# Plain DMAs on the SP queue for the last two stores of a sliding-window kernel, from late buffers

## The chip, the cores and the metric

One core of one Trainium2 chip. The metric is the device time of one execution in microseconds (us). Lower is better.

The names are the profile's. ACT (ScalarE) and DVE (VectorE) copy here; POOL (GpSimd), SP (SyncE) and ACT have queues on which they issue DMAs, which are q0, q1 and q10 in the page. The bytes are moved by 16 DMA engines, packet by packet, between the on-chip buffers and HBM, the memory that holds input and output. A store lands when its last completion is seen. POOL's closing drain is an instruction near the end of the program; in the traces it begins about when POOL issues its last store.

## The reference

```python
# x: (16, 64, 64, 64) float32, window 8, stride 4  ->  out: (16, 15, 15, 64, 8, 8)
for i in range(n_h):                     # n_h = n_w = 15
    for j in range(n_w):
        result[:, i, j] = x[:, :, 4*i:4*i+8, 4*j:4*j+8]
```

It is all copying: 16.8 MB are read and 59 MB are written. In the output one row, of one batch `b`, one window `(i, j)` and one half `ch` of the channels, is 2048 floats, 8 KB in a row. The two halves are neighbours, so a window of one batch is 16 KB.

## The kernel before

Partition `p` holds `(b, ch, q)`, that is 8b + 4ch + q, where `q` is a quarter of the image's rows. A window step `(j, s)` copies, for every partition, the window with `i = 4q + s` into a store buffer and stores the buffer's 128 rows by one indirect DMA of POOL's queue. ACT copies for `s` < 3; for `s` = 3 the window reaches into the next quarter, so DVE copies half and shuffles the other half in from the neighbouring partition. For `s` = 3 the quarter `q` = 3 has no window, and its index is out of bounds on purpose.

```python
UNITS = 18                                     # nine buffers of 1 MB (128 x 2048 f32)
G = gpool.tile([P, UNITS * HCL, WS, WS], f32, name="G")
at = 0
def window(j, s, half):
    # ... u = at % UNITS; at += n        (n = 2 for a whole buffer)
    g = G[:, u * HCL : (u + n) * HCL, :, :]
    if not last:
        nc.scalar.copy(out=g, in_=L[:, cs, s * ST : s * ST + WS, cols])
    else:
        nc.vector.tensor_copy(out=g[:, :, 0:ST, :], in_=L[:, cs, s * ST : RB, cols])
        nc.vector.stream_shuffle(out=g[:, :, ST:WS, :], in_=L[:, cs, 0:ST, cols], mask=nxt)
    # ...
    st = nc.gpsimd.indirect_dma_start(out=o, out_offset=..., in_=g..., ...)
    # ... stores are declared independent of each other
# ... early windows by halves, then
for w in rest:
    window(*w, None)
```

I count stores from the end: store -1 is the last one (`s` = 3, 96 rows), -2 the one before it (`s` = 2, 128 rows).

## Time and profile before

| | before |
|---|---|
| median, lowest to highest | 194.41 us, 194.27 to 194.75 (6 runs, with those beside the changed kernel) |
| span in the profile | 192.4 us |
| last landing of a store | 188.6 us |
| POOL's long drain ends | 191.6 us |

Times within the profile are us from the start of the span. The prediction below shows the lines of the page, of the end in windows and of the closing instructions.

### The profile page before, as it was taken

To read this page: it belongs to the slowest core of one execution; us is meant where nothing else is said; L and a number is where in the kernel's file an instruction comes from. 1 tells how busy PE (TensorE), PEld (TensorE's weight loads), DVE (VectorE), ACT (ScalarE), POOL (GpSimd) and SP (SyncE) were. 2 spreads that over 40 slices of the span, in tenths; PEclk is the share of its full clock that TensorE was granted. 3 is DMA by queue.
4 is the path that set the end of the run, shared out by engine and by line. 5 is a ranking of instruction groups with operands and counts; after the bars stand their busy time and mean duration, and the time that the engine had idled before them with its cause. 6 is when DMAs were issued, how large, how long until landed. Compare 5 with 4: busy or idle time off the path is not lost.

```text
span 192.4 us, 478 instructions
## 1 busy us (share of the span) xinstructions
DVE 30.4 (16%) x65; ACT 86.2 (45%) x55; POOL 70.3 (37%) x77
## 2 busy tenths in 40 slices
DVE  2000050000232302303030122121121203030000
ACT  0000049500699875373747465646565655600000
POOL 0000027723367766456363253434343434440000
DMA  5999999999999999999999999999999999999960
GB/s 183 418 413 410 410 410 414 417 417 422 420 421 427 429 414 429 404 403 418 412 409 409 419 404 409 416 405 409 409 412 409 409 411 412 407 409 414 424 257 17
DMA packets 14724, 75.80 MB, mean 394 GB/s; under 512 B 1984, under 2 KB 1984, under 8 KB 8960
## 3 DMA queue, kind: packets, MB, share of 16 engines
q0 software_dynamic: 10368, 58.99, 75.3%
q1 hardware_dynamic: 2176, 8.39, 11.0%
q10 hardware_dynamic: 2176, 8.39, 10.8%
q14 instruction: 4, 0.03, 0.0%
HBM read 16.78 MB, written 62.91 MB: 414 GB/s over the span
## 4 chain that ended last, share of the span: by engine, by line
DMA 65%; issue 19%; ACT 3%; POOL 1%; POOLq 1%; PEldq 0%
DMA out_dram<-G,idx_last 38%; DMA out_dram<-G,idx 14%; DMA out_dram<-G,idx_h 8%; DMA out_dram<-G,idx_hlast 6%; ACT G L101 3%; POOL out_dram L109 1%; POOLq L165 1%; POOLq L109 0%; POOL pi L61 0%; PEldq L165 0%
## 5 line engine op out<-in xcount | busy, mean ns | idle before, releaser
L101 ACT COPY G<-L 128x2048 f32<-128x2048 f32 (+1 forms) x54 | 84.9, 1613 | 54.4 <-DMA out_dram<-G,idx 18.6
L109 POOL DMA_INDIRECT out_dram<-G,idx x36 | 34.8, 966 | 47.0 <-DMA out_dram<-G,idx 43.1
L103 DVE COPY G<-L 128x1024 f32<-128x1024 f32 (+1 forms) x18 | 11.1, 618 | 138.3 <-DMA out_dram<-G,idx 62.8
L109 POOL DMA_INDIRECT out_dram<-G,idx_h x18 | 17.4, 966 | 13.9 <-DMA out_dram<-G,idx_hlast 4.3
L104 DVE STREAM_SHUFFLE G<-L 128x1024 f32<-128x1024 f32 (+1 forms) x18 | 19.6, 1090 | 0.0
L109 POOL DMA_INDIRECT out_dram<-G,idx_hlast x6 | 5.9, 990 | 27.9 <-DVE G L104 26.4
L109 POOL DMA_INDIRECT out_dram<-G,idx_last x12 | 11.8, 986 | 11.7 <-DVE G L104 6.8
L101 ACT ACT_TABLE_LOAD x1 | 1.3, 1283 | 26.6 <-DMA L<-in_x_dram 26.6
L62 DVE TENSOR_SCALAR tb<-pi 128x1 int32<-128x1 int32 x1 | 0.2, 155 | 1.0 <-POOL pi L61 1.0
L61 POOL IOTA pi<- 128x1 int32 x1 | 0.1, 120 | 0.4 <-PEq L165 0.4
L104 DVE LOAD_MASK_SELECT G<-L x18 | 0.2, 14 | 0.0
L151 POOL MEMSET const-float32-0.0<- 128x1 f32 x1 | 0.1, 100 | 0.2 <-issue 0.2
L68 DVE CUSTOM_DVE_ANT_0 idx<-tb,tc 128x2 uint16<-128x2 uint16 x1 | 0.2, 160 | 0.0
L66 DVE CUSTOM_DVE_ANT_0 tb<-tb,tc 128x2 uint16<-128x2 uint16 x1 | 0.2, 159 | 0.0
L67 DVE TENSOR_SCALAR tc<-tq 128x1 int32<-128x1 int32 x1 | 0.2, 154 | 0.0
L77 DVE TENSOR_SCALAR idx_hlast<-idx_last 128x1 int32<-128x1 int32 x1 | 0.2, 154 | 0.0
L77 DVE TENSOR_SCALAR idx_h<-idx 128x1 int32<-128x1 int32 x1 | 0.2, 154 | 0.0
L71 DVE CUSTOM_DVE_ANT_0 idx_last<-idx,tq 128x2 uint16<-128x2 uint16 x1 | 0.2, 153 | 0.0
L65 DVE TENSOR_SCALAR tb<-tb 128x1 int32<-128x1 int32 x1 | 0.2, 152 | 0.0
L70 DVE TENSOR_SCALAR tq<-tq 128x1 int32<-128x1 int32 x1 | 0.1, 148 | 0.0
L64 DVE TENSOR_SCALAR tq<-pi 128x1 int32<-128x1 int32 x1 | 0.1, 145 | 0.0
L63 DVE TENSOR_SCALAR tc<-pi 128x1 int32<-128x1 int32 x1 | 0.1, 144 | 0.0
(3 smaller groups left out, 0.3 us busy)
## 6 DMA issues: line engine op xcount, KB each, us to landing
L<-in_x_dram ACTq DMA_DIRECT2D x8, 1024.0 KB, 21.1
L<-in_x_dram SPq DMA_DIRECT2D x8, 1024.0 KB, 19.8
out_dram<-G,idx POOLq DMA_INDIRECT x36, 18.2
out_dram<-G,idx_h POOLq DMA_INDIRECT x18, 13.6
out_dram<-G,idx_last POOLq DMA_INDIRECT x12, 18.3
out_dram<-G,idx_hlast POOLq DMA_INDIRECT x6, 13.1
```

Source lines behind the costliest of these rows:

```text
L62: nc.vector.tensor_scalar(out=tb[:, :], in0=pi[:, :], scalar1=3, scalar2=None, op0=ALU.logical_shift_right)
L65: nc.vector.tensor_scalar(out=tb[:, :], in0=tb[:, :], scalar1=float(NWIN * CH), scalar2=None, op0=ALU.mult)
L66: nc.vector.tensor_tensor(out=tb[:, :], in0=tb[:, :], in1=tc_[:, :], op=ALU.add)
L67: nc.vector.tensor_scalar(out=tc_[:, :], in0=tq[:, :], scalar1=float(NSLOT * NW * CH), scalar2=None, op0=ALU.mult)
L68: nc.vector.tensor_tensor(out=idx[:, :], in0=tb[:, :], in1=tc_[:, :], op=ALU.add)
L71: nc.vector.tensor_tensor(out=idx_last[:, :], in0=idx[:, :], in1=tq[:, :], op=ALU.add)
L77: nc.vector.tensor_scalar(out=d[:, :], in0=e[:, :], scalar1=2.0, scalar2=None, op0=ALU.mult)
L101: nc.scalar.copy(out=g, in_=L[:, cs, s * ST : s * ST + WS, cols])
L103: nc.vector.tensor_copy(out=g[:, :, 0:ST, :], in_=L[:, cs, s * ST : RB, cols])
L104: nc.vector.stream_shuffle(out=g[:, :, ST:WS, :], in_=L[:, cs, 0:ST, cols], mask=nxt)
L109: st = nc.gpsimd.indirect_dma_start(out=o, out_offset=bass.IndirectOffsetOnAxis(ap=ix[:, 0:1], axis=0), in_=g.rearrange("p c r w -> p (c r ...
L165: with _tile.TileContext(nc) as tc:
```

## The change

The intent: the last two stores leave by plain DMAs of the SP queue, four for store -2 and three for store -1, one for each quarter `q`. Their buffers are those of stores -5 and -4, so their copies wait until those have landed. The nine buffers become nine tiles.

```diff
+    TAIL, BACK = 2, 3
+    o_q = out.rearrange("b i j (ch cl) r w -> i j b ch (cl r w)", ch=CH)
...
-    G = gpool.tile([P, UNITS * HCL, WS, WS], f32, name="G")
+    G = [gpool.tile([P, 2 * HCL, WS, WS], f32, name=f"G{n}") for n in range(UNITS // 2)]
...
-        g = G[:, u * HCL : (u + n) * HCL, :, :]
+        g = G[u // 2][:, u % 2 * HCL : (u % 2 + n) * HCL, :, :]
...
+        if (j, s) in order[-TAIL:]:
+            g_q = g.rearrange("(m q) c r w -> q m (c r w)", q=HQ)
+            for q in range(HQ - 1 if last else HQ):
+                free(nc.sync.dma_start(out=o_q[q * NSLOT + s, j], in_=g_q[q]))
+            return
...
-    for w in rest:
+    for w in rest[:-TAIL]:
+        window(*w, None)
+    at -= 2 * BACK
+    for w in rest[-TAIL:]:
         window(*w, None)
```

More of the change, by code (lines that the diff above doesn't have):

```diff
@@ L80, with free @@
     nxt = [min(p + 1, 31) for p in range(32)]
+    order = [(j, s) for j in range(NW) for s in range(NSLOT)]
+    TAIL, BACK = 2, 3
+    o_q = out.rearrange("b i j (ch cl) r w -> i j b ch (cl r w)", ch=CH)
+    def free(st):
+        tc.declare_no_dep(st.ins, group="stores", reason="each store writes rows of its own")
+        tc.add_to_no_dep_group("stores", st.ins)
     UNITS = 18
-    G = gpool.tile([P, UNITS * HCL, WS, WS], f32, name="G")
+    G = [gpool.tile([P, 2 * HCL, WS, WS], f32, name=f"G{n}") for n in range(UNITS // 2)]
     at = 0
@@ L117, in window @@
         )
-        tc.declare_no_dep(st.ins, group="stores", reason="each store writes rows of its own")
-        tc.add_to_no_dep_group("stores", st.ins)
-    order = [(j, s) for j in range(NW) for s in range(NSLOT)]
+        free(st)
     EARLY = 12
```

## The prediction

> **What bounds the kernel now.** I read the page's slices first, then the end of the run in windows, then the store issues one by one with their times to landing, then what stands after the last store. The page of the kernel before:
>
> ```profile
> DMA  5999999999999999999999999999999999999960
> GB/s 183 418 413 410 410 410 414 417 417 422 420 421 427 429 414 429 404 403 418 412 409 409 419 404 409 416 405 409 409 412 409 409 411 412 407 409 414 424 257 17
> ```
>
> One slice is 192.4/40 = 4.81 us. From slice 2 to slice 38 the 16 DMA engines are full at some 410 GB/s, so the body is bound by bytes, and the change moves the same bytes. Only the last two slices are free of that bound: 257 and 17 GB/s. The change can act there alone. The same stretch in windows (start:end, length, busy of DVE, ACT and POOL, clock, DMA share, GB/s):
>
> ```profile
> 183.00:184.00 1.00, 0.00 (x0) 0.00 (x0) 0.00 (x0) 1.00 0.97 401
> 184.00:185.00 1.00, 0.00 (x0) 0.00 (x0) 0.00 (x0) 1.00 0.57 238
> 185.00:186.00 1.00, 0.00 (x0) 0.00 (x0) 0.00 (x0) 1.00 0.48 205
> 186.00:187.00 1.00, 0.00 (x0) 0.00 (x0) 0.00 (x0) 1.00 0.47 197
> 187.00:188.00 1.00, 0.00 (x0) 0.00 (x0) 0.00 (x0) 1.00 0.51 213
> 188.00:189.00 1.00, 0.00 (x0) 0.00 (x0) 0.00 (x0) 1.00 0.01 0
> 192.00:193.00 1.00, 0.00 (x0) 0.00 (x0) 0.00 (x0) 1.00 0.00 0
> ```
>
> Two things end the run. From 184 to 188 a share of one half works: eight engines have finished and eight are about 4 us behind. Then from 188.3 to 192.4 no byte moves at all. What stands there is in the list of the closing line of the program (line 165; durations in ns min/median/max, then first and last start):
>
> ```profile
> L165 SPq EVENT_SEMAPHORE  x11: 17/28/28, 188.6 to 192.3; - x11
> L165 POOLq EVENT_SEMAPHORE  x4: 17/17/17, 191.6 to 192.3; - x4
> L165 POOLq DRAIN  x3: 40/107/21281, 170.3 to 192.1; - x3
> L165 SPq DRAIN  x3: 7/7/7, 189.2 to 191.9; - x3
> ```
>
> SP begins to see the completions at 188.6 and its drain is done at 189.2. POOL's drain, begun at 170.3, lasts 21.28 us, to 191.6; the closing barrier follows it (191.6 to 192.4). So POOL's drain ends 2.4 us later than SP's, and about 3.0 us after the last landing. The last landing, from the issue list of the final store:
>
> ```profile
> L109 POOL DMA_INDIRECT out_dram<-G,idx_last x1: 966/966/966, 170.5 to 170.5; - x1
> DMA to landing us min/median/max: 18.1/18.1/18.1
> ```
>
> 170.5 + 18.1 = 188.6. I count stores from the end: this is store -1. In the same way the fifth from the end, store -5, and stores -4 and -3:
>
> ```profile
> L109 POOL DMA_INDIRECT out_dram<-G,idx_last x1: 966/966/966, 161.1 to 161.1; - x1
> DMA to landing us min/median/max: 18.2/18.2/18.2
> ...
> L109 POOL DMA_INDIRECT out_dram<-G,idx x1: 966/966/966, 163.6 to 163.6; - x1
> DMA to landing us min/median/max: 18.3/18.3/18.3
> ...
> L109 POOL DMA_INDIRECT out_dram<-G,idx x1: 966/966/966, 166.0 to 166.0; - x1
> DMA to landing us min/median/max: 18.3/18.3/18.3
> ```
>
> They land at 179.3, 181.9 and 184.3. All is issued by 170.5 and a store takes 18 us to land, eight stores of some 2.5 us each: there is a deep backlog on the engines when POOL has nothing left to do.
>
> **What the Trainium skill says.** "DMA: Bandwidth & Descriptors", section "Issuing engines are not separate DMA queues": DMAs of all issuing engines run on the same 16 engines and interleave. The trace agrees as far as the loads go: they came from two queues and still made 410 to 418 GB/s together. So the SP queue brings no bandwidth. Same page, "Queues, rings and completion order": each DMA engine takes turns between queue rows packet by packet; no run here shows it yet, and I use it for store -3 below. Same page, "Why a DMA increments its semaphore by 16 and not by 1": the engines used by a DMA are the largest number up to 16 that divides the slowest dimension of both sides; here 32 partitions and 16 batches give 16, so plain stores load all engines alike and do not relieve the slow eight. The first-byte latency of 0.6 us for a plain DMA ("Specifications") is less than the trace has: the first load is issued at 0.74 and the first bytes move just after 2.1, so I take 1.4 us. No page that I found says what POOL's drain waits for.
>
> **The change part by part.** *Removed*: two indirect issues on POOL (0.97 us each), which lie under a full DMA queue and are worth nothing by themselves. But with them the last thing that POOL's drain has to wait for becomes store -3. *Tiles*: nine tiles in place of slices of one; same bytes, same depth; in the trace the copies already wait for their own slice, so I give it 0. *Moved*: the copies of stores -2 and -1 must now wait for stores -5 and -4 to land, not for stores nine back. That looks like a loss; its use is that it holds these two behind the POOL queue. Timetable:
>
> 1. Store -5 lands at 179.3; the ACT copy (1.90 us for this form) ends at 181.3. SP issues four plain DMAs of 256 KB; issue of one load took 0.60 us on SP and they followed each other by 0.65, so 181.35 to 183.95. First bytes at 181.35 + 1.4 = 182.8.
> 2. Store -4 lands at 181.9; DVE copy 0.69 + shuffle 1.28 (their rows at 167.9) end at 183.9, just as SP is free. Three DMAs (the fourth has no rows), issued 183.95 to 185.25; last bytes arrive on the queue at 186.7.
> 3. The eight fast engines run out at about 180 (4 us before the others) and idle to 182.8: lost, but they are not the last. They end near 186.7 + 0.6 = 187.3.
> 4. The eight slow engines never idle: at 182.8 they hold 1.2 us of store -3, then 8 + 6 packets of 8 KB. At 418/16 = 26.1 GB/s one packet is 0.314 us, so 182.8 + 1.2 + 14 x 0.314 = 188.4, landing 0.3 later as before: 188.7. Against 188.6 before: nothing gained or lost.
> 5. Store -3 shares the slow engines with store -2 from 182.8; its 1.2 us can double at most, so it lands by about 185.5. If POOL's drain ends 3.0 us after the last landing of its own queue, it ends at 188.5, ahead of SP.
> 6. The end is now SP's: 188.7 + 0.64 (its row of waits, 188.6 to 189.2, as before) = 189.3, plus the closing barrier 192.4 - 191.6 = 0.8: 190.1 to 190.2 in place of 192.4.
>
> Sum: POOL's drain off the end -2.4, the two landings about +0.1: -2.2 to -2.3 us. If SP's wait for the last DMA happens to be late in its row, up to 0.5 more. Time: 194.4 - 2.3 = 192.1 us.
>
> **The rivals.** *The late start costs more than it gives.* If the first bytes of a plain DMA take 3 us, or an SP issue of this shape 1 us, the last DMA reaches the engines after 187.8 and the slow eight idle too: then each us later is a us of the run, and 193 to 195 comes out. For it: the chain landing, copy, issue is serial twice. Against: a slack of 188.4 - 0.6 - 186.7 = 1.1 us by the timetable. *POOL's drain doesn't follow its own queue's last landing* but something else of fixed length or all queues: then the end stays at 191.6 + 0.8 and the time at 194.4. For it: the trace doesn't say what it waits for; against: it outlasts the last landing by 3 us, while another POOL drain took 107 ns. *Rebalancing*: if the plain DMAs gave the idle eight more of the bytes, half of the 4 us lag could go, 2 us more: 190.1. Against: 16 divides both sides, equal shares. *Store -3 is starved by the SP queue* on the slow engines and lands at 187 or later: POOL's drain then ends at 190 and the gain is 1.5 or less: 193.
>
> **Range and chances.** The mechanism with its spread (SP's wait order -0.5, issue and first bytes +1) gives 191.5 to 193.2; the rivals widen it upwards. I predict 192.1 us, with 191.3 to 193.6 as the range for 8 in 10. Two per cent is 3.9 us: under 190.5 only the rebalancing helps, 4 in 100; over 198.3 would need 4 us of idle slow engines, 2 in 100; within 2%, 94 in 100.
>
> **What would show it.** Step 1: ACT's last copy starts near 179.4 and waits for a store with the last-row index. Step 2: DVE's last copy near 181.9. Step 3 and 4: DMA share about one half from 180 to 183, full or nearly from 183 to 187, all bytes moved by 188.4. Step 5: the long POOL drain ends near 188.5. Step 6: SP's closing waits end later than POOL's drain, span 190.1. It is wrong if POOL's drain still ends 2 us or more after SP's, if bytes move after 189.5, or if the body before 179 has changed its length.

## More of the kernel before

The program is on one core, so there is no second die to watch.

## The result, and the profile after

The changed kernel takes 193.37 us (median of 6 runs, 192.94 to 193.51) against 194.41 before: ratio 0.9942, 95% interval 0.9929 to 0.9955. A ratio here is the mean time of one kernel's runs over that of the other's of the same rounds, so it is not quite the ratio of the medians. The gain is clear of noise and is 1.04 us; 2.3 us were predicted.

The page of the changed kernel, the same two rows as before (one slice is now 191.4/40 = 4.79 us):

```profile
DMA  5999999999999999999999999999999999999785
GB/s 180 419 413 410 410 409 413 416 423 420 417 423 429 423 418 425 407 406 414 410 413 404 414 416 413 404 409 409 411 407 409 411 409 406 416 411 416 325 265 187
```

The body is the same to the 37th slice; the last slices now carry bytes to the end, but at 325, 265 and 187 GB/s. The end in windows:

```profile
180.00:181.00 1.00, 0.00 (x0) 1.00 (x1) 0.00 (x0) 1.00 0.48 205
182.00:183.00 1.00, 1.00 (x3) 0.00 (x0) 0.00 (x0) 1.00 0.84 287
183.00:184.00 1.00, 0.62 (x1) 0.00 (x0) 0.00 (x0) 1.00 0.95 279
184.00:185.00 1.00, 0.00 (x0) 0.00 (x0) 0.00 (x0) 1.00 0.71 246
186.00:187.00 1.00, 0.00 (x0) 0.00 (x0) 0.00 (x0) 1.00 0.89 270
188.00:189.00 1.00, 0.00 (x0) 0.00 (x0) 0.00 (x0) 1.00 0.92 311
189.00:190.00 1.00, 0.00 (x0) 0.00 (x0) 0.00 (x0) 1.00 0.50 188
190.00:191.00 1.00, 0.00 (x0) 0.00 (x0) 0.00 (x0) 1.00 0.00 0
```

Read the last two columns together. In the body a DMA share of 1 goes with 410 GB/s. Here shares of 0.89 to 0.95 go with 270 to 311: the engines count as busy, but their packets take longer on average. Bytes move until 190, not 188; the prediction named bytes after 189.5 as a sign of being wrong. The closing instructions (line 165 is now 181):

```profile
L181 SPq EVENT_SEMAPHORE  x11: 17/28/28, 187.4 to 191.4; - x11
L181 POOLq EVENT_SEMAPHORE  x4: 17/17/17, 190.7 to 191.3; - x4
L181 POOLq DRAIN  x3: 40/108/21658, 165.7 to 191.2; - x3
L181 SPq DRAIN  x3: 7/7/7, 190.6 to 190.9; - x3
```

POOL's long drain now ends at 165.7 + 21.7 = 187.4, three us ahead of SP's, at 190.6. SP sets the end, as intended. The copies of the two stores in the timeline, with what they waited for:

```profile
179.21 1.90 ACT L111 COPY G<-L 128x2048 f32<-128x2048 f32 x1 [14.52 <-DMA out_dram<-G,idx_last]
...
181.73 0.69 DVE L113 COPY G<-L 128x1024 f32<-128x1024 f32 x1 [21.24 <-DMA out_dram<-G,idx]
```

And the seven plain stores (issue on SP in ns, first and last issue; then us from issue to landing), and what the SP queue's packets took from 181 to 191 us (packets, MB, share of 16 engines):

```profile
L118 SPq DMA_DIRECT2D out_dram<-G x7: 536/819/1387, 181.1 to 186.2; - x7
...
DMA to landing us min/median/max: 4.0/4.2/4.5
```

```profile
q1 hardware_dynamic: 336, 1.84, 57.8%
```

57.8% of 16 engines over 10 us are 92.5 us; 224 of the 336 packets are 8 KB (the others are 4-byte completions), so one packet takes 0.41 us on average. In the body 410 to 418 GB/s make it 0.31 to 0.32. The average hides two kinds: of the 224 packets in the packed trace, 136 took less than 0.33 us, as in the body, and the other 88 took up to 0.96. Each plain store lands 4 us after its issue. The last is issued at 186.25 and lands at 190.44.

So the bill of the change is: from the last landing to the end of the span, 3.8 us before (192.4 - 188.6) and 1.0 after (191.4 - 190.4), a gain of 2.8; the last landing itself, 188.6 before and 190.4 after, a loss of 1.8. What remains is 1.0.

### The profile page after: what moved, and what is told of

It is laid out like the page before. It is cut to its first block, busy times and chain, and to the rows that moved or that the text cites. A ratio compares the mean times of both kernels' runs of the same rounds, so it can differ in the third digit from the quotient of the medians.

```text
span 191.4 us, 479 instructions
## 1 busy us (share of the span) xinstructions
DVE 30.4 (16%) x65; ACT 86.2 (45%) x55; POOL 68.0 (36%) x75
## 4 chain that ended last, share of the span: by engine, by line
DMA 73%; issue 19%; ACT 2%; POOL 1%; DVE 1%; POOLq 0%; DVEq 0%; PEldq 0%; ACTq 0%
DMA out_dram<-G,idx 60%; DMA out_dram<-G,idx_h 13%; ACT G L111 2%; POOL out_dram L124 1%; DVE G L114 1%; DVE G L113 0%; POOLq L124 0%; POOL pi L61 0%; DVEq L113 0%; PEldq L181 0%; ACTq L111 0%
## 5 line engine op out<-in xcount | busy, mean ns | idle before, releaser
L124 POOL DMA_INDIRECT out_dram<-G,idx x35 | 33.8, 966 | 45.9 <-DMA out_dram<-G,idx 41.7
L124 POOL DMA_INDIRECT out_dram<-G,idx_last x11 | 10.6, 964 | 10.6 <-DVE G L114 5.8
```

What stands on the lines that cost most here:

```text
L124: st = nc.gpsimd.indirect_dma_start(out=o, out_offset=bass.IndirectOffsetOnAxis(ap=ix[:, 0:1], axis=0), in_=g.rearrange("p c r w -> p (c r ...
```

## The experiments

The questions were: does POOL's drain do what I took it to do; does the late start cost anything; is it SP's pace or the packets that make the last landing late; and what makes the packets slow. The theory at first was SP's pace, because seven issues took 0.54 to 1.39 us each where I had counted 0.65; the rival was the engines. "Before" in the ratios is always the kernel before, run in the same rounds.

### The tiles alone

```diff
-    G = gpool.tile([P, UNITS * HCL, WS, WS], f32, name="G")
+    G = [gpool.tile([P, 2 * HCL, WS, WS], f32, name=f"G{n}") for n in range(UNITS // 2)]
```

> The kernel before, with nine tiles in place of slices of one tile and nothing else. Both theories give the tiles nothing: 194.4 us, ratio to before 0.999 to 1.001. If the tiles alone moved a wait, the body before 166 us would change its length and the time with it by over 0.3 us.

Measured: 194.42 us, ratio 1.0006 (0.9992 to 1.0019). The tiles are worth nothing by themselves.

### Plain stores from the usual buffers

```diff
-    at -= 2 * BACK
```

> The changed kernel with its seven plain stores from the usual buffers (nine stores back), so they are issued near 167 and 170 us instead of 181 and 184. If POOL's drain waits for the last landing of POOL's own queue and some 2.9 us more, the plain stores now interleave early, the store third from the end lands last at about 188.3, the drain ends at 191.2 and the time is 194.2 to 194.5, the whole gain gone. If the gain comes from the plain DMAs themselves (fewer POOL issues), it stays: 193.4 or less.

Measured: 197.41 us, ratio 1.0174 (1.0158 to 1.0189), 3 us slower, which neither side had expected. Its closing drain and two windows:

```profile
L180 POOLq DRAIN  x3: 40/108/28827, 166.0 to 195.4; - x3
```

```profile
166.00:170.00 4.00, 1.81 (x3) 1.46 (x1) 0.96 (x1) 1.00 1.02 410
...
174.00:178.00 4.00, 0.00 (x0) 0.00 (x0) 0.00 (x0) 1.00 1.01 356
```

Two things follow. Store -3 landed last on POOL's queue, at 191.95, and the drain ended at 166.0 + 28.8 = 194.9, 2.9 later: the drain part held, and without the late buffers the plain DMAs bring no gain of it. But while plain stores were in flight, the full engines moved 356 GB/s and not 410. The plain stores themselves are slow on the engines, in the middle of a deep backlog, where SP's pace can't matter. That was the first sign against the theory that SP's pace is the cause.

### The late buffers with POOL's indirect stores

```diff
-        if (j, s) in order[-TAIL:]:
+        if False:
```

> The last two stores leave by POOL's indirect DMAs, but from the later buffers, so they start some 12 us later than before. If the late start is free as long as eight engines have a backlog, the last landing stays near 188.6 to 189 and the time is 194.4 to 194.9. If the late start by itself idles the slow engines, the last landing is near 190.4 as in the changed kernel, the drain ends 3 us after it and the time is 196 to 196.5.

Measured: 194.35 us, ratio 1.0002 (0.9988 to 1.0015). The last landing was at 188.73, against 188.62 before, though the last two stores were issued at 181.5 and 184.0 and not at 168.6 and 170.5. The late start is free, as the backlog argument had it. The closing drain:

```profile
L181 POOLq DRAIN  x3: 40/107/7910, 183.8 to 192.2; - x3
```

It began at 183.8 and ended at 191.7, 3.0 after the last landing: its length follows the landing, not its start.

### Two queues

```diff
-                free(nc.sync.dma_start(out=o_q[q * NSLOT + s, j], in_=g_q[q]))
+                free((nc.sync, nc.scalar)[q % 2].dma_start(out=o_q[q * NSLOT + s, j], in_=g_q[q]))
```

> The changed kernel with its seven plain stores alternately on the SP and ACT queues. Theory of the pace: SP issues one 256 KB store each 0.87 us, which is slower than the engines move it, and that sets the last landing; with two queues the last landing moves from 190.4 to 188.8 to 189.4 and the time is 191.8 to 192.5. Rival, the engines: packets of these short stores take 0.42 us on average wherever they are issued from; then the last landing stays at 190.2 to 190.5 and the time at 193.2 to 193.5.

Measured: 192.75 us, ratio 0.9922 (0.9908 to 0.9935); last landing 189.87. That is between the two expectations: 0.57 us of the 1.8 of the last landing come back with a second issuer, 1.2 do not (by the ratios, 0.9942 against 0.9922, 0.4 us of the time). Not all of the 0.57 need be pace: by the same sum as above (29.2% and 24.5% of 16 engines on its two queues) its packets took 0.38 us and not 0.41, and over 14 packets that is 0.4 us. Pace is the smaller part at most. The Trainium skill, "DMA: Bandwidth & Descriptors", section "Issuing engines are not separate DMA queues", says that issuing from several engines only saves issue time, usually small; the small gain here agrees.

### Twice as many plain stores of half the size

```diff
+                for c in range(2):
+                    cc = slice(c * CFREE // 2, (c + 1) * CFREE // 2)
-                free(nc.sync.dma_start(out=o_q[q * NSLOT + s, j], in_=g_q[q]))
+                    free(nc.sync.dma_start(out=o_q[q * NSLOT + s, j][:, :, cc], in_=g_q[q][:, cc]))
```

This is on top of the kernel with the usual buffers.

> The kernel with plain stores from the usual buffers (197.4 us, bytes moved until 191.4 instead of 188.0), with each of its seven plain stores cut into two of half the row: 14 plain DMAs, the same bytes from the same partitions. Theory of a cost for each plain DMA (some 0.5 us of every engine for each): the loss of 3.4 us doubles, 200 to 201.5 us. Theory of a cost for each byte (conflicts of the strided partitions at the ports, or of the rows in HBM): the loss stays, 197.0 to 198.0 us.

Measured: 195.85 us, ratio 1.0083 (1.0069 to 1.0098). The loss did not double, it fell from 3.1 to 1.5 us, outside both expectations. That speaks against a fixed cost for each plain DMA, and so do the packets: what they took beyond normal ones, for each plain store and engine, fell from 0.26 us to 0.10. The size of the loss is not to be read further: 14 issues at up to 2.0 us each stretched to 189.6, so fewer plain bytes met POOL's queue than in the kernel it is compared with.

### Neighbouring partitions

```diff
-                free(nc.sync.dma_start(out=o_q[q * NSLOT + s, j], in_=g_q[q]))
+                g_c = g.rearrange("p c r w -> p (c r w)")[32 * q : 32 * q + 32]
+                free(nc.sync.dma_start(out=o_q[q * NSLOT + s, j], in_=g_c))
```

> The changed kernel, wrong result on purpose: each plain store reads 32 neighbouring partitions instead of every fourth one, and writes the same rows. Sizes, counts, waits and destinations are as in the changed kernel. If conflicts of partitions on the reading side make the plain packets slow, [...]the last landing moves from 190.4 to over 191.2 and the time to 194 or more. If the reading side does not matter: 193.1 to 193.6.

Measured (wrong result): 194.27 us, ratio 0.9997 (0.9984 to 1.0010); last landing 191.37. Its SP queue from 181 to 191 us:

```profile
q1 hardware_dynamic: 334, 1.84, 72.9%
```

The packets took 0.52 us by the same sum. Only the partitions read were changed, so the reading side can slow the packets.

### An earlier start, and one plain store instead of two

```diff
-    TAIL, BACK = 2, 3
+    TAIL, BACK = 2, 4        # back4
+    TAIL, BACK = 1, 3        # one_late
```

> The changed kernel with the buffers of the fourth and third store ahead, so the plain stores start 2.4 us earlier. If lateness and SP's pace are what holds the last landing, it comes 1.5 to 2.4 us earlier (188.4 to 189), the drain of POOL ends near 189 and the time is 191.6 to 192.4. If instead the engines lose time to each plain DMA that meets the POOL queue, the earlier start meets more of it: the last landing stays at 190 or later and the time is 193 to 194.

Measured: 193.08 us, ratio 0.9939 (0.9921 to 0.9957). The plain stores started at 179.4, two us earlier, and the last landing came only 0.2 earlier, at 190.24. An earlier start alone does not help.

> The changed kernel with only the very last store as plain DMAs (three of them), from the buffer of the third store ahead; the store before it goes by POOL as in the kernel before. POOL's last landing is then that store, near 187 (186.8 before, delayed a little by the plain packets), its drain ends 2.9 us later near 190, and the last plain store lands near 189: POOL ends the run, 192.0 to 193.0 us. If each plain DMA costs the engines 0.5 us, three in place of seven save 1 to 2 us of the slow engines' time and the landing of the last one is 188.8 to 189.3.

Measured: 193.28 us, ratio 0.9949 (0.9936 to 0.9962). POOL's last landing, store -2, was delayed from 186.8 to 187.6, its drain ended at 190.54 and ended the run, as expected, though only just after SP's own closing drains (190.44 and 190.50); the time is 0.3 us above the expected range. Even three plain stores landed late: the last landed at 190.05, not near 189.

### Where the bytes go to: scratch in place of the output

Three kernels in which the plain stores write to a scratch area in HBM, the first of them 32 rows in a row. Their outputs are wrong, which doesn't matter for the times.

```diff
+    scr = nc.dram_tensor("scratch", (2, P, CFREE), f32, kind="Internal").ap()
-                free(nc.sync.dma_start(out=o_q[q * NSLOT + s, j], in_=g_q[q]))
+  strided:      free(nc.sync.dma_start(out=scr[s - 2, 32 * q : 32 * q + 32], in_=g_q[q]))
+  own:          free(nc.sync.dma_start(out=scr[s - 2, :, cc], in_=g_c[:, cc]))   # cc: a quarter row, all 128 partitions
+  one:          one DMA of 128 x 2048 for store -2, one of 128 x 1536 for store -1
```

> Control, wrong result on purpose: the changed kernel, its seven plain stores of 256 KB read the same strided partitions but write to a scratch area in HBM, 32 rows in a row, instead of to the output. If the rows written play no part, it repeats the changed kernel: last landing 190.0 to 190.7, time 193.0 to 193.5 us. If the spread of the rows in HBM is what slows the plain packets, it is 192.4 or less.

> As scr_strided (scratch, wrong result on purpose), but each plain store reads all 128 partitions and a quarter of their row, in place of 32 strided partitions and the whole row: same number of plain stores, same bytes each, packets of 2 KB. If conflicts on the reading side (two engines reading the same group of partitions at once) make the plain packets slow, the last landing moves to 188.6 to 189.4 and the time to 191.6 to 192.5. If SP's pace of issue or the count of plain stores is what holds it, nothing moves: 193.0 to 193.6.

> As scr_own, but each of the last two stores is one plain DMA (1 MB and 0.75 MB, all 128 partitions): two plain DMAs in place of seven. Both the pace of SP and the reading conflicts are gone, so this is what the prediction took the plain path to be: last landing 188.5 to 189.1, time 191.5 to 192.2. If a plain store is slow for another cause (the HBM write, the sharing with the POOL queue), it stays above 192.8.

Measured: 191.59, 191.65 and 191.77 us; ratios 0.9853 (0.9839 to 0.9868), 0.9853 (0.9840 to 0.9865) and 0.9864 (0.9850 to 0.9879). The control, meant to repeat the changed kernel, was the surprise: same partitions, same seven issues from SP, and 1.7 us faster by the ratios. Its SP queue and its windows:

```profile
q1 hardware_dynamic: 336, 1.84, 44.3%
...
scratch<-G SPq DMA_DIRECT2D x7, 256.0 KB, 3.0
```

```profile
185.00:186.00 1.00, 0.00 (x0) 0.00 (x0) 0.00 (x0) 1.00 0.99 410
186.00:187.00 1.00, 0.00 (x0) 0.00 (x0) 0.00 (x0) 1.00 0.87 361
187.00:188.00 1.00, 0.00 (x0) 0.00 (x0) 0.00 (x0) 1.00 0.96 401
188.00:189.00 1.00, 0.00 (x0) 0.00 (x0) 0.00 (x0) 1.00 0.07 25
```

44.3% over 224 packets are 0.316 us for one, and none of the 224 took 0.33 or more: the plain packets now move at the body's speed, a plain store lands 3.0 us after issue in place of 4.2, and the last landing is 188.84. This is the timetable of the prediction. With two issues in place of seven (the third kernel) the last landing is 188.56 and the time is no better: at normal packets SP's pace costs nothing.

### What it is about the destination

```diff
+  spread: scr (B, NWIN * CH * CFREE), seen as (w, b, ch, f)     # the output's spacing, another tensor
+  pad:    the same, each batch 1024 floats longer
+  near:   scr (2 * HQ, B, CH + 1, CFREE)[.., 0:CH]              # pairs of rows with a gap, near together
+  gap32:  scr (2 * HQ, 32, 2, CFREE)[.., 0]                     # single rows, each followed by a gap
```

> Wrong result on purpose: as scr_strided (191.6 us), but the scratch area has the output's layout: 16 batches 3,686,400 bytes apart, two rows of 8 KB each, so 16 engines write at the output's spacing at once, into another tensor. If the spacing of the rows written together is what makes the plain packets slow, it repeats the changed kernel: packets of 0.40 us, 192.9 to 193.6 us. If it is the output tensor itself (rows that POOL's stores write next to them), it stays at 191.4 to 191.9.

> Wrong result on purpose: as scr_spread, with each batch of the scratch area 4096 bytes longer. If 16 rows at one offset from multiples of 16 KB fall on the same part of HBM, the pad spreads them: 191.4 to 191.9 us. If only the distance counts, whatever its lower bits: as scr_spread.

> Wrong result on purpose: as scr_strided, but the scratch rows lie as pairs of 8 KB with a gap of 8 KB after each pair, so that the DMA has the same three-dimensional form as the changed kernel's (16 by 2 by 2048), near together. If the form of the DMA is what slows it: 192.9 to 193.6 us. If the far spacing does: 191.4 to 191.9.

> Wrong result on purpose: as scr_strided, but each scratch row is followed by 8 KB of gap, so nothing is contiguous, yet the DMA has the two-dimensional form 32 by 2048. scr_near differed from scr_strided in gaps and in form. If the gaps are the cause, packets of 0.40 us and 193 to 193.5 us; if the form (16 by 2 by 2048) is, packets of 0.312 us and 191.4 to 191.9.

Measured: spread 193.41, pad 193.41, near 193.32, gap32 191.61 us; ratios 0.9950 (0.9937 to 0.9963), 0.9951 (0.9936 to 0.9966), 0.9946 (0.9934 to 0.9959), 0.9855 (0.9840 to 0.9870). The SP queue from 181 to 191 us, first in near, then in gap32:

```profile
q1 hardware_dynamic: 336, 1.84, 58.3%
```

```profile
q1 hardware_dynamic: 336, 1.84, 44.4%
```

So it is neither the tensor, nor the 3.7 MB between batches, nor (for a pad of 4 KB) their address bits, nor gaps. What the slow ones share is the form of the DMA: 16 batches by 2 rows by 2048. The fast ones are 32 rows by 2048 (or 128 rows). Everything else may be the same, the partitions read included.

### Does the form act through the reading side

```diff
+  scr_contig: free(nc.sync.dma_start(out=scr[s - 2, 32 * q : 32 * q + 32], in_=g_c[32 * q : 32 * q + 32]))
+  by_ch_two:  for ch in range(CH):       # correct: one row for each of 16 batches, halves on two queues
+                  free((nc.sync, nc.scalar)[ch].dma_start(out=o_q[q * NSLOT + s, j, :, ch], in_=g_q[ch * HQ + q]))
```

> Wrong result on purpose: as scr_strided (form 32 by 2048, compact scratch), but each plain store reads 32 neighbouring partitions. If the form acts only through what it costs to generate, it stays at 191.4 to 191.9 us. If it acts through which partitions are read by which engine at once, this crowding slows the packets in the good form as it did in the other (contig, 0.52 us): 192.6 us or more.

> A correct kernel: the changed kernel with each plain store cut by channel half, so that each DMA has the form 16 by 2048 (16 batches, one row of 8 KB each); the two halves go on the SP and ACT queues, 14 plain DMAs in all. If the three-dimensional form is what slows the packets, they take 0.312 us again, the last landing falls to 188.5 to 189.2 and the time to 191.5 to 192.3 us, the best correct version. If what matters is which group of partitions each engine reads (here every second group in each DMA), the packets stay at 0.4 us or more and the time is 192.6 or more, that of two_queues.

Measured: scr_contig 194.26 us, ratio 0.9995 (0.9981 to 1.0009); by_ch_two, correct, 193.31 us, ratio 0.9941 (0.9928 to 0.9955), last landing 190.6. The SP queue of scr_contig, from 181 to 191 us (its last packets come after 191):

```profile
q1 hardware_dynamic: 327, 1.84, 74.7%
```

That is 0.53 us a packet in the good form: against scr_strided only the partitions read differ, and the price is 2.7 us. And by_ch_two has a two-dimensional form and yet 0.41 us a packet (32.5% and 24.8% of 16 engines on its two queues). So three dimensions are not needed for slow packets, and crowded reading is enough. By_ch_two and the slow form share 16 as their outermost count, where the fast ones have 32 or 128; no run parts that from the rest. The Trainium skill, "SBUF — State Buffer", section "Door 1: The DMA port swizzle", has the map: 32 neighbouring partitions reach 8 of the 16 ports, and by its formula so do the 16 partitions of one DMA of by_ch_two, which are 8 apart (its two queues reach a different eight each, so this is the weaker witness). The trace agrees in kind for the 32 neighbouring ones: 0.53 us a packet in place of 0.316. The 32 strided partitions of the changed kernel reach all 16. There the order might do it: if each engine takes one batch, the 16 engines read partitions 8b + q first and 8b + 4 + q next, eight ports at a time. That last step is argued, not shown, since no record names the engine of a packet.

The packets in the trace don't fit this step as it stands. On each engine the two rows of a plain store follow each other without a gap, with the 4-byte completion behind them, and 108 of the 112 pairs of the changed kernel can be told in this way. The first row took 0.50 us on average and only 28 of 108 were normal (under 0.33); the second took 0.309 in 107 of 108. By that step both rows would be slow. With crowded reading both are slow: in scr_contig 150 of the 224 packets took longer than 0.33, so second rows are among them. For one common cause speaks that the two don't add: contig has both the slow form and neighbouring partitions, and its packets took 0.52 where scr_contig's took 0.53. A cost at the start of each engine's part of a DMA of this form would fit the slow first rows too; no run tests it.

### An earlier start on two queues

```diff
-    TAIL, BACK = 2, 3
+    TAIL, BACK = 2, 4        # with the two queues of two_queues
```

> Buffers of the fourth and third store ahead and the seven plain stores alternately on SP and ACT. If pace and start both count, the last landing falls below that of two_queues (189.9), to 188.9 to 189.6, POOL's own last landing is near 186 and its drain ends near 189: 191.9 to 192.6 us. If the plain packets that meet the POOL queue cost the slow engines as much as the early start gives, it is 192.6 to 193.1.

Measured: 193.38 us, ratio 0.9962 (0.9931 to 0.9992), last landing 190.38, by the median worse than two_queues from the later buffers (0.9908 to 0.9935; the intervals just touch). The expectation's second case, and beyond it. The likely reason, not parted from others, is that more of the slow packets meet POOL's queue. The best correct version of all is two_queues, 192.75 us. No run wrote the output itself in one of the fast forms.

## Why the prediction was right or wrong

POOL's drain (the 2.4 us of the sum) was right, and the rival that it follows something else is out. In eight traces the drain ends 2.90 to 2.99 us after the last landing of POOL's own queue:

| kernel | last landing of POOL's queue | drain ends | between |
|---|---|---|---|
| before | 188.62 | 191.61 | 2.99 |
| changed | 184.48 | 187.39 | 2.91 |
| usual_buffers | 191.95 | 194.86 | 2.91 |
| usual_halves | 190.00 | 192.90 | 2.90 |
| pool_late | 188.73 | 191.72 | 2.99 |
| two_queues | 184.95 | 187.86 | 2.91 |
| back4 | 185.89 | 188.80 | 2.91 |
| one_late | 187.60 | 190.54 | 2.94 |

- Step 1 was right: store -5 landed at 179.1, ACT's copy began at 179.21, the first plain store was issued at 181.14 and its first bytes moved at 182.45 (predicted 181.35 and 182.8).
- Step 2 was right for the copies (DVE from 181.73 to 183.62) and off for SP: the last issue began at 186.25, not 185.25, since issues took 0.54 to 1.39 us. Even with normal packets single issues took up to 1.18 (scr_strided), so the loads were a poor measure of it; there it had no price.
- Step 3 was right on the idle eight (share 0.48 at 180 to 181) and wrong on their end, as step 4 tells.
- Step 4 failed, and it is the step that decides. It gave the 14 plain packets of each slow engine "At 418/16 = 26.1 GB/s one packet is 0.314 us", from the rate of the body. They took 0.41. The last landing was 190.4 and not 188.7, 1.75 us late. The mis-sized term, 14 packets, is 1.4 of that (14 x 0.1); the other 0.35 isn't parted further, but the engines were not always busy either (share 0.71 at 184 to 185). The claim that only the slow eight count fell with it: all 16 engines finished the last plain store within 0.6 us, 189.84 to 190.44, where the fast eight were to end near 187.3. With packets of 0.316 us (scr_strided) the step's figures come back: 188.84, and 191.6 us.
- Step 5 was right in kind: store -3 landed at 184.5, earlier than the 185.5 allowed for.
- Step 6 was right, with the favourable order of SP's waits that it left open: SP's drain was done 0.2 us after the last landing, not 0.64. So of the 1.75 us lost, 0.45 came back: 190.15 + 1.75 - 0.45 = 191.45, the span of 191.4.

Of the rivals, the first (the late start costs) had the right sign, but its reason is refuted: pool_late starts as late and pays nothing, and SP's pace accounts at most for the 0.57 us of the last landing that a second queue recovers; with normal packets (scr_one against scr_strided) fewer issues recover nothing in the time. Equal shares for all 16 engines, on which I dropped rebalancing, agree with 16 completion packets for each plain store (336 = 7 x 48). What I passed over is that equal bytes for every engine do not make equal speed: which partitions they read at once counts too.

What stays open: why the 16 by 2 by 2048 form slows its packets, and how it shares its rows over the engines. That the form decides is shown (near against gap32). That reading crowded partitions slows packets is shown (scr_contig against scr_strided). That the first is an instance of the second is only argued, and the slow first and normal second rows speak against its simple version.

## What to carry to other kernels

Here the last stores went by POOL's queue, and its closing drain kept the run open for 3 us after the last landing; let another queue carry the last bytes, and hold these back until POOL's backlog is nearly gone, which was free here while eight engines still had work (pool_late). Do not price such a plain DMA at the rate of the body: look at the share and the GB/s of its stretch together, since a nearly full share at 280 GB/s meant slow packets here. And before blaming the destination or the issuing engine, write the same bytes to a scratch area in another form; here that told more than the runs that changed the schedule.

## What the Trainium skill lacked or had wrong

- No page that I found says what POOL's closing drain waits for: here it ends 2.90 to 2.99 us after the last landing of POOL's own queue, in eight traces, whatever other queues still move.
- "DMA: Bandwidth & Descriptors", "Why a DMA increments its semaphore by 16 and not by 1", says how many engines a DMA uses, but not which rows each gets where there are not 128 partitions: two forms with 16 engines each and the same partitions took 0.316 and 0.41 us a packet of 8 KB.
- Same page, "Specifications": about 0.6 us to the first byte of a plain DMA, without saying from where it is counted; here it took, from the start of the issue, 1.45 us for the first load (0.74 to 2.19) and 1.31 for the first plain store (181.14 to 182.45), and from the end of the issue 0.78 and 0.71.
- Same page, "Issuing engine by pattern", calls the plain path generally faster: here the last store landed at 188.7 by POOL from the late buffers (pool_late) and at 190.4 by the plain DMAs from the same buffers; in the faster form, to scratch, it was 188.8.
